# Two feed-forward units ordered by a table, squares moved into the loop, first projection by kind, first cast on VectorE

## The chip, the cores and the metric

The kernel runs on one core of one Trainium2 chip. The metric is the device time of one execution in microseconds (us); the kernel before was run three times: 2028.01, 2030.51 and 2027.96 us, median 2028.01. Engines are named as in the profile: PE is TensorE (PEld its weight loads), DVE VectorE, ACT ScalarE, POOL GpSimd, SP the queue that issues most transfers.

## What is computed

One transformer block on a sequence of 512 rows of 2048 columns, in float32. Cut to what matters here:

```python
h = rmsnorm(x, g_attn)
proj = h @ w_in                       # q, k, v of 16 heads and the forget gates
...                                   # two kinds of attention, head norms
x = x + mixed @ w_out
h2 = rmsnorm(x, g_mlp)
u = relu(h2 @ w_up)                   # 2048 -> 8192
x = x + (u * u) @ w_down              # 8192 -> 2048
y = rmsnorm(x, g_final)
```

## The kernel before

**Products of float32.** TensorE is fed with operands split in two: a high part, which ScalarE makes by a rounding copy ("cast"), and a low part, the source less the high part, which VectorE makes ("low"). A product is then three matmuls, high by high (hh), high by low (hl) and low by high (lh), in `mm3` (lines 75 to 78). Split operands of weights go to rotating rooms (`hi_lo`, line 67): three of them, and more where `more_parts` has entries.

**Seven products for eight.** The large products are done as one level of Winograd's scheme: two by two blocks on both sides, seven products numbered 1 to 7 instead of eight, with sums of blocks on either side. Sums of weights are made in place by VectorE (`Unit.source`, `sums_ahead`), sums of the left side by `a_source`; `left_form` and `a_form` split a sum of the left side into its high and low form `F[p]`.

**Three places matter here.**

*The first projection (lines 212 to 444).* x comes in as 16 chunks of 128 columns. For chunk k, `turn_x` transposes it on TensorE into one of two banks; from that bank ScalarE writes hH (`x_high`), VectorE hL (`x_low`), and further copies and sums are taken for later products (`x_more` on VectorE; `x_right` on ScalarE and `x_sum` on VectorE for chunks 8 to 15). The bank is free for the chunk after next when all of them have read it. Then the chunk is multiplied with its rows of the first weights: `first_part` does all four row blocks of one kind, hh, hl or lh, with the three kinds at 0, 0.6 and 1.1 us of the plan; `first_values` does two row blocks with the three kinds in turn. The first eight chunks of `seq` use `first_part`, the last eight `first_values`. `keep_busy(n)` puts n dummy matmuls into a spare bank. `square_x` takes sums of squares of x on ScalarE. The whole stage is a `Plan`: a list of jobs with times, sorted by time and then traced, inside a block where TensorE, ScalarE, VectorE and SP keep the order of the trace (`manual_schedule`). The times only order the jobs; nothing waits for a clock. The next stage, the values of the other heads, begins with products of pieces named `q` into the bank `vx`.

*The first two feed-forward units (lines 1612 to 1636).* A unit is 256 columns of w_up. Units 0 and 1 are multiplied while the last left forms are still being made, as plain products of 24 matmuls each into banks A, B and C (`psa`, `psb`, `psc`), in the order 1, 2 for each unit and then 5, 6, 7, 4, 3 with the units in turn. `product` makes the split, multiplies and calls `finish`, which copies banks out on ScalarE, adds them on VectorE, and after product 3 applies Relu and Square to the unit's result c. Before, the planner of the language orders these instructions by its own model, held back in places by `issue_after`. The last quarter of x, `quarter[1, 0]`, is turned in between (`turn_quarter`), stored to `xd`, and its squares are taken in place (`take_squares`).

*The loop over the other units (lines 1709 to 1749).* Steps of 16 matmuls, one product each, in an order fixed by hand on TensorE, ScalarE and VectorE: at step k the cast of step k + 3, the low of step k + 2, the sum of step k + 4 (`step_cast`, `step_low`, `step_source`), the copies and sums of step k - 1, Relu and Square of a finished unit one per step (`later`), and the forms of finished pairs of units, which are stored to memory for the down projection (`todo`, `going`, `form_low`: seven forms for a pair, each a sum where there is one, a cast, a low and a store). Loads of w_up go to `rw`, five rooms; the result c of units 0 and 1 takes one of them until its forms are made. SP is not held to an order here.

Of the kernel before, what the change touches and what calls it, by code (L numbers as in the profile page):

```python
# [14 lines left out]
P = 128  # L15
# [21 lines left out]
def block_kernel(ctx, tc, x, g_attn, w_in, b_f, g_out_sb, g_out_fox, w_out, g_mlp, w_up, w_down, g_final, y):  # L37
# [117 lines left out]
    class Piece:  # L155
# [13 lines left out]

        def low(self):  # L170
            lows[0] = dve.tensor_tensor(self.lo, self.source(), self.hi.bitcast(F32), op=ALU.subtract)
# [40 lines left out]
    with ExitStack() as stage:  # L212
# [82 lines left out]
        def first_part(j, piece, i, part):  # L295
            for t in range(TB):
                ts = slice(t * P, (t + 1) * P)
                a, b = (hH[j], piece.hi) if part == "hh" else (hH[j], piece.lo) if part == "hl" else (hL[j], piece.hi)
                pe.matmul(first_ps[t][:, :m], a[:, ts], b[:, i, :], start=j == 0 and part == "hh", stop=False, skip_group_check=True)
# [43 lines left out]
        for j in seq[:8]:  # L343
            for part, wait in zip(("hh", "hl", "lh"), (0.0, 0.6, 1.1)):
                plan.at(mm_at[j] + wait, first_part, j, *pieces[j], part)
        plan.at(-58.0, keep_busy, 9)
        plan.at(-54.5, keep_busy, 1)
        plan.at(1.0, keep_busy, 5)
        early = {0: ((-5.0, turn_x), (-4.1, "cast"), (-4.0, x_high), (-3.9, "low"), (-3.5, x_low), (-3.3, x_more)),
# [4 lines left out]
                 10: ((-2.36, turn_x), (-1.4, x_high), (-0.7, x_low), (0.05, x_sum), (0.55, x_right)),  # L354
# [8 lines left out]
        for k in range(4, K8):  # L363
            t, j = mm_at[k], k + K8
            for jj, dt in ((k, 0.0), (j, step)):
                for half in range(2):
                    plan.at(t + dt + 0.74 * half, first_values, jj, *pieces[jj], half)
# [792 lines left out]

    class Unit:
        def __init__(self, u):
            self.u = u
            cols = slice(2 * u * P, 2 * (u + 1) * P)
            rows_ = w_up.rearrange("(a i p) f -> i p a f", i=2, p=P)
            self.rows = rows_[0][:, :, cols], rows_[1][:, :, cols]
            self.b = []
            if u >= 2:
                self.load(0)
                self.load(1)  # L1170
            self.A = None
            self.both = u >= 2
            self.summed = False
# [7 lines left out]
        def sums_ahead(self):  # L1181
            (b11, b12), (b21, b22) = self.b
            dve.tensor_tensor(b11, b12, b11, op=ALU.subtract)
            dve.tensor_tensor(b12, b22, b12, op=ALU.subtract)
            self.summed = True

        def source(self, p):
# [5 lines left out]
            if p == 4:  # L1193
                with ExitStack() as order_:
                    if self.summed:
                        order_.enter_context(tc.issue_after(lows[0].ins))
                    dve.tensor_tensor(b21, b21, b11, op=ALU.subtract)
# [40 lines left out]
        def product(self, p):  # L1238
            ins = self.multiply(p, self.parts(p))
            self.finish(p)  # L1240
            return ins

# [35 lines left out]
        def finish(self, p):  # L1278
            if self.both:
                self.copies(p)  # L1280
                self.sums(p)
                if p == 3:
                    for _ in self.squares():
                        pass
                return
            if p == 2:
                if self.u % 2 == 0:
                    hidden[0] = rw.tile([P, 2, 2, NT], F32, tag="rw", name="c")
                self.pair = hidden[0]
                self.c = hidden[0][:, self.u % 2]  # L1290
            t1, t2 = slice(0, 2 * P), slice(2 * P, NT)
            if p in (1, 6, 7):
# [4 lines left out]
                if p == 1:  # L1297
                    self.m1 = self.m
            if p == 7:
                dve.tensor_tensor(self.c[:, 1, t2], self.m, self.C, op=ALU.add)  # L1300
            if p == 2:
                dve.tensor_tensor(self.c[:, 0, t1], self.m1, self.B, op=ALU.add)
            if p == 4:
                act.copy(self.c[:, 0, t2], self.A)
            if p == 3:
                dve.tensor_tensor(self.c[:, 1, t1], self.m6, self.C, op=ALU.add)
                act.activation(self.c, self.c, AF.Relu)
                act.activation(self.c, self.c, AF.Square)
# [67 lines left out]

    def turn_quarter(t0, j, db):
# [4 lines left out]
        for a in range(2):  # L1382
            tr = trp.tile([P, 2, 2 * P], F32, tag="tr", name="tr1")
            for i in range(2):
                for t in range(2):
                    pe.transpose(tr[:, i, t * P:(t + 1) * P], x_[:, t, (2 * a + i) * P:(2 * a + i + 1) * P], ident)
            for i in range(2):
                k = 4 * n + 2 * a + i
                act.mul(hr[db][j][:, a, i, t0 * 2 * P:(t0 + 1) * 2 * P], tr[:, i, :], g_up[:, k:k + 1])
# [5 lines left out]
    def take_squares():  # L1395

        t0, n, x_ = squares.pop(0)
        for t in range(2):
            act.activation(x_[:, t, :], x_[:, t, :], AF.Square, accum_out=ss2[:, 2 * t0 + t, n:n + 1])
# [7 lines left out]
    for db in range(2):  # L1407
# [204 lines left out]
    ins = units[0].multiply(1, begun[0])  # L1612
    with tc.issue_after(ins.ins):
        turn_quarter(1, 0, 1)
    units[0].multiply(2, begun[1])
    units[0].finish(1)
    units[0].finish(2)
    for p in (1, 2):
        ins = units[1].product(p)
    for unit in units[:2]:  # L1620
        unit.sums_ahead()
    left_form(4, 1, 0)
    left_form(5, 1, 0)
    for p in (5, 6, 7, 4, 3):
        for j in range(2):

            with tc.issue_after(ins.ins):
                ins = units[j].product(p)
            q = {5: 6, 6: 7, 7: 3}.get(p)
            if q is not None:  # L1630

                with tc.issue_after(lows[0].ins):
                    if (q, j) != (6, 0):
                        left_form(q, 1, 1 - j)
    while squares:
        take_squares()
# [15 lines left out]
    todo += [(q, hidden[0], 0) for q in A_ORDER]  # L1652
# [45 lines left out]
    going, later, pair_next = [], [], None  # L1698
# [10 lines left out]
    with tc.manual_schedule(engines={pe.engine, act.engine, dve.engine}):  # L1709
        for k in range(3):  # L1710

            for step in (step_source, step_cast, step_low):
                step(k)
        step_source(3)
        for k in range(len(steps)):
# [29 lines left out]
            if n in (1, 3, 6, 5 if steps[k][0] % 2 else 2) or steps[k][0] < 4:  # L1745
# [250 lines left out]
```

## Time and profile before

| what | value |
|---|---|
| median of three runs | 2028.01 us |
| the profiled execution | 2029.46 us |
| its span, first to last instruction | 2027.7 us |
| DVE, ACT busy | 1739.6 and 1128.6 us |
| HBM traffic | 315.19 MB read, 96.49 MB written |
| first projection | about 6.5 to 39.5 us of the span |
| units 0 and 1 | about 775.9 to 818.4 us |
| loop over the other units | from 818.4 us |

A row of a timeline gives the start in us, the duration in us, the engine, the line, the operation, what it writes and reads, shapes, a count, and in brackets how long the engine had been idle before it and what ended that. Matmuls overlap, so their spacing is read from the starts. A row of waits gives the total in us, how often, and the longest. Rows of windows give the busy time of each engine and the number of its instructions in a stretch.

### The profile page before, as it was taken

The page shows a single profiled execution, that of the slowest core. Times are in us where ns is not written, and L with a number is a line of the kernel's source. Part 1 is how long each engine was busy: PE and PEld are TensorE (multiplying, and loading weights), DVE is VectorE, ACT ScalarE, POOL GpSimd, SP SyncE. Part 2 cuts the span into 40 slices and gives each one's busy share as a digit, 9 for nine tenths or more (in the row PEclk, how much of TensorE's full clock was granted, in tenths as well). Part 3 has the DMA queues.
Part 4 walks back from the last instruction along what each step waited for, and adds up shares of the span by engine and source line. Part 5 has one row for each costly group of instructions (what it writes and reads, how often), then busy time and mean ns, then how long its engine had stood idle before and what let it go on. Part 6 is the DMA issues. An engine that isn't in the chain of part 4 may idle for free.

```text
span 2027.7 us, 27207 instructions
## 1 busy us (share of the span) xinstructions
PE 2016.1 (99%) x10425; PEld 1745.7 (86%) x10425; DVE 1739.6 (86%) x1970; ACT 1128.6 (56%) x1619; POOL 63.6 (3%) x72
## 2 busy tenths in 40 slices
PE   9999999999999999999999999999999999999998
PEld 9998888888898889888888888888888888888886
DVE  7886777888868588999999999998798888888896
ACT  7544444555555556666767767676644344444344
POOL 0000110100000000000000000000000000000004
PEclk9999999999999999999999999999999999999999
DMA  7427656666648981666676666666785574674642
GB/s 241 165 72 253 216 189 196 192 210 184 192 140 275 300 270 64 220 185 198 197 217 187 209 207 190 215 196 241 254 312 191 220 265 167 231 256 175 217 159 84
DMA packets 270179, 413.46 MB, mean 204 GB/s; under 512 B 10280, under 2 KB 165976, under 8 KB 263520
## 3 DMA queue, kind: packets, MB, share of 16 engines
q1 hardware_dynamic: 269296, 409.61, 60.7%
q8 instruction: 82, 1.34, 0.3%
q10 hardware_dynamic: 752, 2.11, 0.3%
q14 instruction: 49, 0.40, 0.1%
HBM read 315.19 MB, written 96.49 MB: 203 GB/s over the span
## 4 chain that ended last, share of the span: by engine, by line
PE 95%; DVE 3%; ACT 1%; issue 1%; DMA 0%; ACTq 0%
PE psa L1229 10%; PE accd L78 8%; PE accd L77 8%; PE accd L76 8%; PE accq L76 6%; PE accq L78 6%; PE accq L77 6%; PE psa L1227 5%; PE psc L1229 5%; PE psc L1227 3%; PE psb L1229 3%; PE m L77 1%; PE m L78 1%; PE m L76 1%; PE psb L1227 1%; PE vy L78 1%
## 5 line engine op out<-in xcount | busy, mean ns | idle before, releaser
L1806 ACT CAST wh<-wd 128x1024 fp32r<-128x1024 f32 x126 | 125.1, 999 | 168.2 <-PE accd L78 55.1
L1696 DVE TENSOR_TENSOR wl<-wu,wh 128x1024 fp32r<-128x1024 f32 x158 | 192.6, 1220 | 13.0 <-ACT wh L1690 13.0
L76 PE MATMUL accq<-hH,wh 128*128 128x512 f32 x512 | 201.4, 393 | 0.0
L78 PE MATMUL accq<-hH,wl 128*128 128x512 f32 x512 | 199.7, 390 | 0.0
L77 PE MATMUL accq<-hL,wh 128*128 128x512 f32 x512 | 199.6, 390 | 0.0
L1690 ACT CAST wh<-wu 128x1024 fp32r<-128x1024 f32 x158 | 167.4, 1060 | 44.8 <-issue 22.6
L1229 PE MATMUL psa<-f,wh 128*128 128x512 f32 x720 | 179.0, 391 | 0.0
L77 PE MATMUL accd<-wl,uf 128*128 128x512 f32 x436 | 169.6, 389 | 0.0
L78 PE MATMUL accd<-wh,uf 128*128 128x512 f32 x436 | 169.6, 389 | 0.0
L76 PE MATMUL accd<-wh,uf 128*128 128x512 f32 x436 | 169.4, 389 | 0.0
L1229 PEld LDWEIGHTS psa<-f,wh 128*128 128x128 f32 x720 | 132.3, 188 | 25.6
L1813 DVE TENSOR_TENSOR wl<-wd,wh 128x1024 fp32r<-128x1024 f32 x126 | 144.0, 1151 | 10.6 <-ACT wh L1806 10.6
L1578 DVE TENSOR_TENSOR m<-m,accd 128x1024 f32<-128x1024 f32 x84 | 102.2, 1217 | 47.7 <-PE accd L78 47.7
L1806 ACT CAST wx<-wd 128x1024 fp32r<-128x1024 f32 (+1 forms) x82 | 80.8, 995 | 107.4 <-PE accd L78 43.5
L78 PEld LDWEIGHTS accq<-hH,wl 128*128 128x128 f32 x512 | 96.1, 188 | 20.1
L77 PEld LDWEIGHTS accq<-hL,wh 128*128 128x128 f32 x512 | 96.2, 188 | 18.6
L76 PEld LDWEIGHTS accq<-hH,wh 128*128 128x128 f32 x512 | 96.3, 188 | 18.5
L76 PE MATMUL accd<-wx,uf 128*128 128x512 f32 x284 | 110.5, 389 | 0.0
L77 PE MATMUL accd<-wx,uf 128*128 128x512 f32 x284 | 110.5, 389 | 0.0
L78 PE MATMUL accd<-wx,uf 128*128 128x512 f32 x284 | 110.5, 389 | 0.0
L168 ACT CAST wh<-wraw 128x1024 fp32r<-128x1024 f32 (+1 forms) x70 | 72.8, 1041 | 60.1 <-PE accq L77 51.2
L1227 PEld LDWEIGHTS psa<-f,wl 128*128 128x128 f32 x720 | 96.0, 191 | 5.9 <-ACT l L1260 0.6
(445 smaller groups left out, 5104.2 us busy)
## 6 DMA issues: line engine op xcount, KB each, us to landing
wu<-in_w_up_dram SPq DMA_DIRECT2D x60, 1024.0 KB, 6.5
ufd<-st SPq DMA_DIRECT2D x98, 512.0 KB, 3.8
wd<-in_w_down_dram SPq DMA_DIRECT2D x48, 1024.0 KB, 8.3
uf<-ufd SPq DMA_DIRECT2D x42, 1024.0 KB, 6.7
wraw<-in_w_in_dram SPq DMA_DIRECT2D x68, 512.0 KB, 4.1
wo<-wsums SPq DMA_DIRECT2D x28, 512.0 KB, 5.0
q<-in_w_in_dram SPq DMA_DIRECT2D x32, 384.0 KB, 6.3
wd<-in_w_down_dram SPq DMA_DIRECT2D x16, 768.0 KB, 5.8
```

The source lines that it names most:

```text
L76: pe.matmul(out, sh, mh, start=first, stop=False, skip_group_check=True)
L77: pe.matmul(out, sh, ml, start=False, stop=False, skip_group_check=True)
L78: return pe.matmul(out, sl, mh, start=False, stop=last, skip_group_check=True)
L168: act.copy(self.hi, self.source())
L1227: ins = pe.matmul(ps[:, 2 * P:], lo[:, a, :], f_parts(p, a)[0], start=False, stop=last, skip_group_check=True)
L1229: ins = pe.matmul(ps, hi[:, a, :], f_both(p, a), start=a == PAIRS[0] and p in (1, 5), stop=last, skip_group_check=True)
L1578: dve.tensor_tensor(M[p][:, :, db, :], M[p][:, :, db, :], ps, op=ALU.add)
L1690: act.copy(rooms[k][0], srcs[k])
L1696: lows[0] = dve.tensor_tensor(lo, srcs.pop(k), hi.bitcast(F32), op=ALU.subtract)
L1806: act.copy(rooms[k + 3][0], srcs[k + 3])
L1813: dve.tensor_tensor(rooms[k + 2][1], srcs.pop(k + 2), rooms[k + 2][0].bitcast(F32), op=ALU.subtract)
```

## The change

1. The high part of the weights of chunk 0 is made by VectorE (`cast_dve`) instead of ScalarE, and one dummy matmul of five before the first product is dropped.
2. `first_values` is gone: all 16 chunks are multiplied by `first_part`, one kind after the other.
3. `x_right` of chunk 10 stands directly behind its `x_high` instead of 1.85 us later in the plan.
4. Units 0 and 1 become a `Plan` of their own, with every cast, low, sum, multiply, copy and addition at a time, in a block that holds TensorE, ScalarE and VectorE to the order. `finish` is split for these units into `copied` (ScalarE) and `added` (VectorE). The transposes of the last quarter come after the second product instead of between the first and the second, and its squares later among the casts. The left sum of product 7 for the second half is made ahead of the first products.
5. The addition after product 3 of units 0 and 1 is made among the first lows of the loop, and their Relu and Square go through the loop's list, one per step. The forms of this pair are queued only after them, and the rule by which the first units' steps each took a form is dropped.

```diff
+        def cast_dve(self):
+            self.hi, self.lo = (w.rearrange("p (a b) -> p a b", a=self.a) for w in hi_lo(self.a * self.b))
+            dve.tensor_copy(self.hi, self.source())
...
-                pe.matmul(first_ps[t][:, :m], a[:, ts], b[:, i, :], start=j == 0 and part == "hh", stop=False, skip_group_check=True)
-
-        def first_values(j, piece, i, half):
-            for t in (2 * half, 2 * half + 1):
-                ts = slice(t * P, (t + 1) * P)
-                mm3(first_ps[t][:, :m], hH[j][:, ts], hL[j][:, ts], piece.hi[:, i, :], piece.lo[:, i, :], j == 0, j == KC - 1)
+                pe.matmul(first_ps[t][:, :m], a[:, ts], b[:, i, :], start=j == 0 and part == "hh", stop=j == KC - 1 and part == "lh", skip_group_check=True)
...
-        for j in seq[:8]:
+        for j in seq:
...
-        plan.at(1.0, keep_busy, 5)
-        early = {0: ((-5.0, turn_x), (-4.1, "cast"), (-4.0, x_high), (-3.9, "low"), (-3.5, x_low), (-3.3, x_more)),
+        plan.at(1.0, keep_busy, 4)
+        early = {0: ((-5.0, turn_x), (-4.1, "cast_dve"), (-4.0, x_high), (-3.9, "low"), (-3.5, x_low), (-3.3, x_more)),
...
-                 10: ((-2.36, turn_x), (-1.4, x_high), (-0.7, x_low), (0.05, x_sum), (0.55, x_right)),
+                 10: ((-2.36, turn_x), (-1.4, x_high), (-1.3, x_right), (-0.7, x_low), (0.05, x_sum)),
...
+            with tc.issue_after(lows[0].ins):
+                summed[7, 1, 1] = a_source(7, hr[1][1])
             with tc.issue_after(casts[0].ins):
                 begun = [units[0].parts(1), units[0].parts(2)]
+            for p in (5, 7):
+                units[0].sum_ahead(p)
...
+    plan, groups = Plan(), {}
+    last = (1, 0, 1)
+    plan.at(-2.9, units[0].multiply, 1, begun[0])
+    plan.at(0.0, units[0].multiply, 2, begun[1])
+    for a in range(2):
+        plan.at(2.95, lambda a=a: groups.update({a: turn_group(*last, a)}))
+        plan.at(4.05 + 0.95 * a, lambda a=a: take_group(*last, a, groups[a]))
+        plan.at((14.0, 19.7)[a], lambda a=a: take_square(1, 1, quarter[1, 0], a))
+    plan.at(2.96, lambda: sp.dma_start(xd[1][:, 2:4, :], quarter[1, 0]))
+
+    for u, p, begin_, total, cast, low in (
+            (1, 1, 3.8, None, -1.9, -0.8), (1, 2, 6.7, None, 0.5, 3.4), (0, 5, 9.75, None, 3.0, 4.65), (1, 5, 12.45, None, 7.2, 8.5),
+            (0, 6, 16.05, 10.4, 11.65, 12.85), (1, 6, 18.2, 11.6, 12.9, 14.8), (0, 7, 21.1, None, 15.6, 17.4), (1, 7, 24.0, None, 18.6, 19.3),
+            (0, 4, 26.9, 20.5, 21.8, 23.0), (1, 4, 29.8, 21.75, 24.4, 25.1), (0, 3, 32.7, None, 27.3, 29.2), (1, 3, 35.6, None, 30.2, 30.9)):
+        w = FirstProduct(u, p)
...
+    for p, j, total, cast, low in ((7, 1, None, -1.0, 1.5), (4, 0, None, 5.95, 7.1), (5, 0, 7.8, 8.45, 9.7), (6, 0, 14.1, 14.85, 16.0),
+                                   (7, 0, 16.7, 17.45, 18.6), (3, 1, 24.2, 25.5, 26.35), (3, 0, 27.0, 28.4, 28.5)):
+        w = Left(p, j)
...
+    for t, f, u, p in ((0.1, "copied", 0, 1), (6.2, "added", 0, 2), (6.8, "copied", 1, 1), (12.5, "added", 1, 2), (18.25, "copied", 0, 6),
+                       (21.15, "copied", 1, 6), (24.05, "copied", 0, 7), (24.9, "added", 0, 7), (26.95, "copied", 1, 7),
+                       (27.7, "added", 1, 7), (29.85, "copied", 0, 4), (32.75, "copied", 1, 4)):
+        plan.at(t, getattr(units[u], f), p)
+    for t, p in ((2.2, 5), (5.9, 7)):
+        plan.at(t, units[1].sum_ahead, p)
+    with tc.manual_schedule(engines={pe.engine, act.engine, dve.engine}):
+        plan.run()
...
-    todo += [(q, hidden[0], 0) for q in A_ORDER]
...
-    going, later, pair_next = [], [], None
+    going, later, pair_next = [], [w.squares() for w in units], units[1]
...
+            if k == 2:
+                units[0].added(3)
             for step in (step_source, step_cast, step_low):
                 step(k)
...
             step_cast(k + 3)
+            if k == 0:
+                units[1].added(3)
...
             if later and next(later[0], 1):
-                later.pop()
+                later.pop(0)
...
-            if n in (1, 3, 6, 5 if steps[k][0] % 2 else 2) or steps[k][0] < 4:
+            if n in (1, 3, 6, 5 if steps[k][0] % 2 else 2):
                 form_low()
```

The new classes `Left` and `FirstProduct` hold one job each: `sum` is the sum of blocks (VectorE), `cast` the high part (ScalarE), `low` the low part (VectorE), `multiply` the 24 matmuls. In the first list of the table, the columns are unit, product, and the times of multiply, sum, cast and low.

More of the change, by code (lines that the diff above doesn't have):

```diff
@@ L1159, in a_form @@
         split(*out, a_source(p, c, s))
+    summed = {}
     class Unit:
@@ L1278, in finish, with copied @@
         def finish(self, p):
[L1279 to L1291, printed above, removed]
+            self.copies(p)
+            self.sums(p)
+            if p == 3:
+                for _ in self.squares():
+                    pass
+        def copied(self, p):
             if p in (1, 6, 7):
@@ L1382, in turn_quarter @@
         for a in range(2):
[L1383 to L1389, printed above, removed]
+            take_group(t0, j, db, a, turn_group(t0, j, db, a))
         sp.dma_start(xd[n][:, 2 * t0:2 * t0 + 2, :], x_)
@@ L1609, in block_kernel @@
     old = None
[L1612 to L1634, printed above, removed]
@@ L1635, in block_kernel, with __init__, sum, cast @@
-    while squares:
-        take_squares()
+    class Left:
+        def __init__(self, p, j):
+            self.p, self.c, self.at = p, hr[1][j], slice(2 * j, 2 * j + 2)
+        def sum(self):
+            self.src = a_source(self.p, self.c)
+        def cast(self):
+            if self.p == 4:
+                self.sum()
+            if F[self.p][1] is None:
+                F[self.p][1] = form.tile([P, 4, 2, 2 * P], F32R, tag=f"fl{self.p}", name=f"f{self.p}")
+            self.out = [F[self.p][1][:, self.at, c, :] for c in range(2)]
+            act.copy(self.out[0], self.src)
+        def low(self):
+            lows[0] = dve.tensor_tensor(self.out[1], self.src, self.out[0].bitcast(F32), op=ALU.subtract)
@@ new lines, in block_kernel, with __init__, sum, cast @@
+    class FirstProduct:
+        def __init__(self, u, p):
+            self.unit, self.p, self.src = units[u], p, None
+        def sum(self):
+            self.src = self.unit.source(self.p)
+        def cast(self):
+            if self.src is None:
+                self.sum()
+            self.parts = self.unit.room(self.p)
+            act.copy(self.parts[0], self.src)
+        def low(self):
+            lows[0] = dve.tensor_tensor(self.parts[1], self.src, self.parts[0].bitcast(F32), op=ALU.subtract)
+        def multiply(self):
+            self.unit.multiply(self.p, self.parts)
@@ new lines, in block_kernel @@
+    plan, groups = Plan(), {}
[8 more added lines that the diff above has]
+    for u, p, begin_, total, cast, low in (
[3 rows of a table added]
+        w = FirstProduct(u, p)
+        if total is not None:
+            plan.at(total, w.sum)
+        for t, f in ((cast, w.cast), (low, w.low), (begin_, w.multiply)):
+            plan.at(t, f)
```

60 lines of the change are left out of this document (37 added, 23 removed).

## The prediction

> **What bounds the kernel now.** I read the page's shares first, then the chain, then what TensorE and its weight loads (PEld) waited for over the whole span, and last the timelines around those few waits.
>
> ```profile
> PE 2016.1 (99%) x10425; PEld 1745.7 (86%) x10425; DVE 1739.6 (86%) x1970; ACT 1128.6 (56%) x1619; POOL 63.6 (3%) x72
> PE 95%; DVE 3%; ACT 1%; issue 1%; DMA 0%; ACTq 0%
> PEld psa L78 <- DVE wl L59: 1.0, 2, 0.5
> PEld vy L78 <- DVE hL L262: 0.6, 3, 0.2
> PEld psa L1227 <- ACT l L1260: 0.6, 1, 0.6
> PEld tr L256 <- ACT x L268: 0.4, 1, 0.4
> ...
> ```
>
> TensorE is busy 99% of the span, and the chain that ended last is 95% TensorE. So work taken off another engine is worth nothing in itself; only a TensorE gap can be won. 2027.7 less 2016.1 leaves 11.6 us without a matmul, head and tail included, and the waits (total us, times, longest) name four gaps that lie where the edits are: at most 2.6 us. That is the first answer: this change can win two or three microseconds, about 0.1%.
>
> ```profile
> core 0: us, PE busy (x) PEld busy (x) DVE busy (x) ACT busy (x) POOL busy (x), PEclk, DMA share, GB/s
> 10.20:39.46 29.26, 29.00 (x237) 28.20 (x237) 25.35 (x41) 23.16 (x42) 0.00 (x0) 1.00 0.75 268
> 32.00:36.00 4.00, 3.98 (x34) 3.77 (x33) 4.00 (x7) 2.78 (x5) 0.00 (x0) 1.00 0.54 186
> 775.90:818.40 42.50, 41.86 (x347) 41.46 (x346) 37.57 (x47) 24.58 (x39) 0.00 (x0) 1.00 0.34 109
> ```
>
> The third stretch is the two units that go into the table: 347 matmuls in 42.5 us, 0.12 us each, with VectorE at 37.57 of 42.5 and ScalarE at 24.58. Neither is full there; only their order can hurt.
>
> **The change part by part. First weights cast on VectorE, four dummy matmuls for five.**
>
> ```profile
> 4.39 1.05 PE L256 MATMUL tr<-ident,xa 128*128 128x128 f32 x4
> 6.50 0.81 PE L299 MATMUL vy<-wh,hH 128*128 128x264 f32 x2
> 8.84 0.64 PE L299 MATMUL vz<-wl,hH 128*128 128x264 f32 x2
> 9.28 0.64 PE L299 MATMUL vy<-wh,hL 128*128 128x264 f32 x2
> 5.45 0.41 ACT L168 CAST wh<-wfirst 128x264 fp32r<-128x264 f32 x1 [2.88 <-DMA wfirst<-in_w_in_dram]
> 5.77 0.68 ACT L259 ACTIVATE hH<-tr,g_in 128x512 fp32r<-128x512 f32 x1
> 1.23 0.29 DVE L289 CAST still<-f 128x256 fp32r<-128x256 f32 x1
> 5.89 0.43 DVE L171 TENSOR_TENSOR wl<-wfirst,wh 128x264 fp32r<-128x264 f32 x1 [1.60 <-ACT wh L168]
> ```
>
> The first product starts at 6.50, when the high part of x is done (5.77 + 0.68 = 6.45). That instruction stood behind the cast of the weights; x itself was turned by 4.39 + 1.05 = 5.44. On VectorE, idle for 1.60 us there, the cast costs about 0.3 (nearest row: 256 columns in 0.29) and ends near 5.8, when wl could start before as well. ScalarE then starts at about 5.46, and the product at 6.18, 0.32 earlier; the dropped dummy matmul makes room for that. But matmuls in this stretch start 0.22 apart (8.84 to 9.28 for two) against 0.12 later, so 0.32 us of them is 0.32 x 0.12 / 0.22 = **0.17** of later time, if the pace still changes at the same moment. Bounds: 0 (if the VectorE cast delays wl) and 0.32.
>
> [...]
>
> **x_right of chunk 10 right behind its x_high.**
>
> ```profile
> 19.41 0.40 PE L299 MATMUL vz<-wh,hL 128*128 128x264 f32 x2
> 20.03 0.66 PE L256 MATMUL tr<-ident,xa 128*128 128x128 f32 x4 [0.22 <-ACT x L268]
> 19.50 0.48 ACT L268 ACTIVATE x<-tr,g_in 128x256 f32<-128x256 f32 x1
> ```
>
> Turning chunk 11 needs the bank of chunk 10, whose last reader is this x_right at 19.50. TensorE loses 20.03 - 19.41 - 2 x 0.12 = **0.38**. Moved ahead of a square and a cast, x_right ends near 17.5, and nothing else reads the bank so late. Queued behind it on ScalarE, the square and the next x_high (18.39) slip by some 0.2, and that chunk's product starts only after 20; on VectorE, chunk 10's x_low slips by up to 0.3, and its lh are the last of the chunk (the row at 19.41). Both are covered. Bounds: 0 and 0.38.
>
> **All chunks by kind.** The last eight chunks ran hh, hl, lh for each pair of blocks; now every chunk runs its four hh, then four hl, then four lh.
>
> ```profile
> 36.17 0.28 PE L77 MATMUL vy<-wl,hH 128*128 128x264 f32 x1
> 36.48 0.39 PE L78 MATMUL vy<-wh,hL 128*128 128x264 f32 x1
> 29.37 0.75 DVE L262 SCALAR_TENSOR_TENSOR hL<-tr,g_in,hH 128x512 fp32r<-128x512 f32 x1 [0.23 <-ACT x L268]
> 37.34 0.75 DVE L262 SCALAR_TENSOR_TENSOR hL<-tr,g_in,hH 128x512 fp32r<-128x512 f32 x1 [0.26 <-ACT x L268]
> 38.40 1.82 DVE L171 TENSOR_TENSOR wl<-q,wh 128x768 fp32r<-128x768 f32 x2
> ```
>
> The third matmul of a chunk waited for hL: 36.48 - 36.17 - 0.12 = 0.19 here, three times in all, so **0.5** by the longest (PEld says 0.6). By kind, hL is wanted at the ninth matmul, 6 x 0.12 = 0.7 us later than at the third, and every one of these waits is under 0.2. The number of matmuls and their 0.12 stay. Bounds: 0.3 and 0.6.
>
> What is late next is VectorE: full from 32 to 36 (4.00 of 4.00), it makes the first wl of the next stage at 38.40, done at 38.40 + 1.82 / 2 = 39.31; TensorE begins that stage at 39.46 and needs wl one matmul later. Coming 0.17 + 0.38 + 0.5 = 1.05 earlier it would want wl at about 38.6. If VectorE did not move, 0.7 would be given back. But both ends of its full run wait on ScalarE (0.23 at 29.37, 0.26 at 37.34), and ScalarE there waits for the turned chunk from TensorE: the run moves with TensorE by about 0.55 at its head, and the gap at its end takes the rest. I take **0.05** given back; bounds 0 and 0.7.
>
> **The two units in a table.**
>
> ```profile
> 805.89 0.28 PE L77 MATMUL psa<-f,wh 128*128 128x256 f32 x1
> 806.46 0.38 PE L78 MATMUL psa<-f,wl 128*128 128x256 f32 x1 [0.29 <-DVE wl L59]
> 802.80 1.22 DVE L1197 TENSOR_TENSOR wu<-wu 128x1024 f32<-128x1024 f32 x1
> 818.44 2.00 PE L1229 MATMUL psa<-f,wh 128*128 128x512 f32 x8
> ```
>
> Product 4 of each unit waits for wl, 806.46 - 805.89 - 0.12 = 0.45, twice: **0.9**. Its sum was started on VectorE only at 802.80. In the table sum, cast and low of unit 0's product 4 stand 6.4, 5.1 and 3.9 us ahead of its multiply. The work is the same (12 casts, 12 lows, 7 left forms and so on), so VectorE's 37.57 of 42.5 stays. Of the leads, added up from durations in the table's order, the thinnest is this: low of left form (5, 0) comes after some 9.5 us of VectorE work from -0.8, ending about 10.5, and is wanted by the 19th matmul of product (0, 5) at 9.75 + 18 x 0.12 = 11.9; every other low stands two or more us ahead. Rooms: each cast comes after the multiply three before it, by the table. The transposes of the last quarter move from between the first two products to behind them, the same eight; its two squares wait for the store of x, issued at about 3 on SP, which the table does not order, and stand at 14.0 and 19.7. Bounds: 0 (another instruction is late in the new order) and 1.0 (the PEld row).
>
> **Squares and left forms in the loop.**
>
> ```profile
> 843.55 1.98 PE L1229 MATMUL psa<-f,wh 128*128 128x512 f32 x8
> 848.12 0.42 DVE L1269 TENSOR_TENSOR c<-c,psc 128x256 f32<-128x256 f32 x1
> 853.56 1.06 ACT L1276 ACTIVATE c<-c 128x1024 f32<-128x1024 f32 x1
> 855.20 0.98 PE L1227 MATMUL psa<-f,wl 128*128 128x256 f32 x6 [0.37 <-ACT l L1260]
> 825.45 0.69 DVE L1508 TENSOR_TENSOR st<-c,st 128x512 fp32r<-128x512 f32 x1 [0.51 <-ACT st L1506]
> 843.99 0.68 DVE L1508 TENSOR_TENSOR st<-c,st 128x512 fp32r<-128x512 f32 x1
> ```
>
> Nine steps of the loop take 843.55 - 818.44 = 25.1, 2.79 each. VectorE adds a finished bank (848.12) 4.6 us after TensorE left it (843.55): it has made the seven forms of the first pair one per step, 825.45 to 843.99. Relu and Square follow late on ScalarE, the copies stand behind the Square of 853.56, and TensorE loses 0.37. With the condition on steps below 4 gone, forms come at four per unit, begin at the fourth step (behind two Relu and two Square at one per step) and end near the 15th, 818.44 + 15 x 2.79 = 860. By step 8 three instead of seven are done: four times 0.68, and the sums before three of them, off VectorE, over 3 us of the 4.6. So the **0.37** goes. The two additions into c now stand on VectorE between the loop's first lows, and block them until the last table products end: then sum, cast, low of step 2 (1.2 + 1.0 + 1.2) are done some 4 us on, against 5.6 until TensorE's third step. Bounds: -0.5 (the forms now crowd steps 8 to 15) and 0.4.
>
> **The sum:** 0.17 + 0.38 + 0.5 - 0.05 + 0.9 + 0.37 = 2.27, so the span goes from 2027.7 to 2025.4 and the profiled execution from 2029.46 to 2027.2. The median of the three runs, 2028.01, lies 1.45 below the profiled one; taken from it, **2025.7 us**. Nothing between 40 and 775 or after 870 eats it: TensorE has next to no waits there.
>
> **The rivals.**
>
> 1. *VectorE sets the end of the first stage.* For: 4.00 of 4.00 busy there. Against: its run starts and ends on ScalarE waits that come earlier. It gives back 0.7 instead of 0.05: 2028.01 - 1.6 = 2026.4.
> 2. *The table gains nothing*, because only the order is fixed and another low comes as late as the old one. For: VectorE 88% busy. Against: the leads above. Without the 0.9 and the 0.37: 2027.0.
> 3. *The pace changes earlier* relative to the first product. For: the slow stretch from 6.50 to about 10.2 costs 3.7 x (1 - 0.12 / 0.22) = 1.7 us that no row ties to the edit. Against: nothing in the edit moves it on purpose. 2025.7 - 1.7 = 2024.0.
> 4. *Slower: weight loads queue behind form stores on SP.* The loop's loads and the stores of forms share SP in order, and the forms move from steps 1 to 7 into steps 4 to 15, where the fifth room of the weights also stays with c.
>
> ```profile
> 840.62 0.38 SPq L1179 DMA_DIRECT2D wu<-in_w_up_dram  x1
> wu<-in_w_up_dram SPq DMA_DIRECT2D x60, 1024.0 KB, 6.5
> ```
>
> The load at 840.62 is unit 4's second half, there at 847.2, and its first reader (a sum for step 16, taken at step 12) comes at 818.44 + 12 x 2.79 = 851.9: 4.7 us of cover. Unit 5's second half loses c's room and must wait for unit 3's, at about 858, there at 864.5 against 871.4. If a load stands behind a store whose form is one place later, two steps, 5.6 us, TensorE loses 0.9; from 4.7 + 2.3 = 7.0 us on the kernel is slower than before, and with two such places, 11.2 us, it loses 6.5: 2028.01 - 2.3 + 6.5 = 2032.2. Against: the loads become ready by VectorE's own pace, which is better now.
>
> **How the numbers follow.** Forecast 0.56 (2024.6 to 2026.9 by its bounds and the runs' spread), rival 1 0.13, rival 2 0.10, rival 3 0.10, rival 4 0.11. A measurement of this kernel can tell about 0.2%, 4.06 us, from no change: 2023.95 to 2032.07. Half of rival 3 lies below, with a little of the forecast: faster 0.07. Rival 4 is above in most of its cases: slower 0.08. Same 0.85. The range takes the forecast, rivals 1 and 2 and most of 3: 2023.9 to 2029.2; the upper end leaves room for the spread of the runs (those before reach 2030.51).
>
> **What would show it.** First product near 6.2 with the same 0.22 spacing up to about 10; no TensorE gap before the transposes at about 19.6 and none at third matmuls of chunks; the next stage starting near 38.5, with or without a wait for wl (rival 1). The two units ending about 41.6 us after they begin instead of 42.6, with no weight load waiting for wl. VectorE's addition of a bank at the ninth step within about 1.5 us of TensorE's end instead of 4.6, and no wait behind L1260. A TensorE wait on a load of wu in the 40 us after the loop begins would make rival 4 right, a span over 2027.7 would make the whole sum wrong.

## The result, and the profile after

| | before | after |
|---|---|---|
| median, 15 runs each | 2028.59 us | 2024.33 us |
| lowest to highest | 2027.82 to 2030.51 us | 2024.07 to 2024.92 us |
| ratio, 95% interval | | 0.9979 (0.9971 to 0.9987) |
| the profiled execution, its span | 2029.46, 2027.7 us | 2024.44, 2022.7 us |

The changed kernel is 4.26 us faster, 0.21%, where 2.3 us were forecast: the direction and the range held, but the forecast was little more than half of the gain. The page after, with busy times and the chain, then what TensorE's weight loads waited for over the whole span:

```profile
PE 2013.0 (100%) x10424; PEld 1743.7 (86%) x10424; DVE 1739.4 (86%) x1971; ACT 1127.2 (56%) x1618; POOL 63.1 (3%) x72
PE 100%; ACT 0%; DVE 0%; issue 0%; ACTq 0%
```

```profile
PEld vx L297 <- DVE still L293: 1.6, 1, 1.6
PEld trg L252 <- issue: 0.5, 2, 0.2
PEld trb L719 <- DVE rw L714: 0.4, 1, 0.4
PEld accoa L78 <- DVE g L59: 0.4, 1, 0.4
PEld tr L260 <- issue: 0.3, 1, 0.3
PEld vy L303 <- ACT hH L263: 0.2, 1, 0.2
```

The chain is now TensorE alone. The waits for hL, for the weights' low parts in the units (psa L78) and for the copies in the loop are all gone. One row is new: tr L260 is a short wait before the next transposes, those of chunk 4 (the run e8 below is about it). No wait for a load of wu has come in.

Where the time came from is read by cutting the span at the same five matmuls in each kernel: the first product, chunk 1's first product, chunk 11's transposes, the first matmul of the next stage, the first of the units, the first of the loop; the last piece ends with TensorE. The windows of the changed kernel (bounds, length, busy us and instructions of each engine), then the first and last matmul of the loop's piece and the last store:

```profile
core 0: us, PE busy (x) PEld busy (x) DVE busy (x) ACT busy (x) POOL busy (x), PEclk, DMA share, GB/s
6.23:8.57 2.34, 2.34 (x18) 2.32 (x17) 1.79 (x4) 0.93 (x2) 0.00 (x0) 1.00 1.04 321
8.57:18.15 9.58, 9.58 (x82) 9.53 (x81) 8.32 (x15) 7.81 (x15) 0.00 (x0) 1.00 1.06 390
18.15:36.93 18.78, 18.61 (x159) 18.43 (x157) 17.59 (x28) 15.47 (x29) 0.00 (x0) 1.00 0.73 247
773.40:814.81 41.41, 41.41 (x347) 41.41 (x346) 36.99 (x46) 23.65 (x38) 0.00 (x0) 1.00 0.35 113
814.81:2014.71 1199.90, 1199.90 (x6086) 1026.28 (x6084) 1100.31 (x1147) 681.98 (x954) 20.13 (x14) 1.00 0.62 208
...
```

```profile
814.81 2.00 PE L1225 MATMUL psa<-f,wh 128*128 128x512 f32 x8
2014.43 0.28 PE L78 MATMUL acce<-ws,us 128*128 128x256 f32 x1
2018.34 0.39 ACTq L1977 DMA_DIRECT2D out_dram<-last  x1
```

In the units and in the loop TensorE is busy for every hundredth of the stretch: 41.41 of 41.41 and 1199.90 of 1199.90. In the stretch from 18.15 a hole of 0.17 us is left. The end of the profile before:

```profile
2018.68 0.28 PE L78 MATMUL acce<-ws,us 128*128 128x256 f32 x1
2022.62 0.40 ACTq L1922 DMA_DIRECT2D out_dram<-last  x1
```

TensorE ends 4.25 us earlier. The span shrank by 5.0: from the issue of the last store to the end it is 2022.7 - 2018.34 = 4.4 us now and 2027.7 - 2022.62 = 5.1 before, which no step of the prediction had.

The lengths of all pieces, for these two profiles and for those of the experiments below (the stretch between the next stage and the units is 736.4 to 736.5 us in all but one, 736.7):

| profile | first product to chunk 1 | chunk 1 to 11 | 11 to next stage | units | loop to TensorE's end | last store to end |
|---|---|---|---|---|---|---|
| before | 3.66 | 9.87 | 19.43 | 42.56 | 1200.52 | 5.12 |
| e9_before | 2.49 | 9.97 | 19.43 | 43.03 | 1200.53 | 5.16 |
| e10_before | 2.00 | 10.06 | 19.44 | 43.14 | 1200.54 | 5.12 |
| e1_start | 2.49 | 9.61 | 18.77 | 42.91 | 1200.51 | 4.36 |
| e2_units | 2.01 | 10.78 | 19.43 | 41.41 | 1199.90 | 4.36 |
| e3_cast | 2.00 | 9.97 | 19.45 | 43.05 | 1200.50 | 5.11 |
| e4_kind | 2.44 | 9.60 | 18.78 | 42.90 | 1200.51 | 4.37 |
| e5_xright | 2.31 | 9.61 | 19.74 | 42.61 | 1200.68 | 4.35 |
| e6_forms | 1.99 | 10.09 | 19.44 | 42.92 | 1199.90 | 4.38 |
| after | 2.34 | 9.58 | 18.78 | 41.41 | 1199.90 | 4.38 |
| e12_after | 2.22 | 9.61 | 18.75 | 41.41 | 1199.90 | 4.37 |
| e11_old_head | 2.58 | 9.59 | 18.75 | 41.42 | 1199.89 | 4.38 |
| e7_old_forms | 2.61 | 9.58 | 18.77 | 41.42 | 1201.13 | 4.66 |
| e8_bank | 2.42 | 9.61 | 18.40 | 41.41 | 1199.90 | 4.36 |

In the new order the pieces repeat within 0.04 us, and so do the third column (19.43 to 19.45) and the loop (1200.50 to 1200.54) of the old order; the one exception in the loop is e5 with 1200.68, for which no further gap on TensorE was found. In such a column an edit's effect shows to the tenth. The first column doesn't repeat at all. In the old order the second runs from 9.87 to 10.09, with one 10.78, and the units' from 42.56 to 43.14.

### The profile page after: what moved, and what is told of

It reads as the page before. It is cut to its first block, busy times and chain, and to the rows that moved or that the text cites. A ratio compares the mean times of both kernels' runs of the same rounds, so it can differ in the third digit from the quotient of the medians.

```text
span 2022.7 us, 27206 instructions
## 1 busy us (share of the span) xinstructions
PE 2013.0 (100%) x10424; PEld 1743.7 (86%) x10424; DVE 1739.4 (86%) x1971; ACT 1127.2 (56%) x1618; POOL 63.1 (3%) x72
## 4 chain that ended last, share of the span: by engine, by line
PE 100%; ACT 0%; DVE 0%; issue 0%; ACTq 0%
PE psa L1225 11%; PE accd L76 8%; PE accd L78 8%; PE accd L77 8%; PE accq L76 6%; PE accq L78 6%; PE accq L77 6%; PE psa L1223 6%; PE psc L1225 5%; PE psc L1223 3%; PE psb L1225 3%; PE psb L1223 1%; PE m L76 1%; PE m L78 1%; PE m L77 1%; PE accoa L78 1%
## 5 line engine op out<-in xcount | busy, mean ns | idle before, releaser
L78 PE MATMUL accq<-hH,wl 128*128 128x512 f32 x512 | 199.7, 390 | 0.0
L78 PE MATMUL accd<-wh,uf 128*128 128x512 f32 x436 | 169.6, 389 | 0.0
L78 PEld LDWEIGHTS accq<-hH,wl 128*128 128x128 f32 x512 | 96.1, 188 | 20.2
L78 PE MATMUL accd<-wx,uf 128*128 128x512 f32 x284 | 110.5, 389 | 0.0
```

The source lines that it names most:

```text
L78: return pe.matmul(out, sl, mh, start=False, stop=last, skip_group_check=True)
```

## The experiments

Each was timed beside the kernel before on the same chip, in five rounds (11 runs each, before 21 or 33) except e9 and e10, one run each. The medians of the kernel before were 2028.58 for e1 to e4, 2028.54 for e5 to e8, 2028.50 for e9 to e12. The times of e1, e3, e4, e5 and e6 have intervals that reach 1 or nearly so; for these the stage lengths carry the reading, not the ratio.

**The two halves apart.** e1 is the kernel before with the edits to the first projection alone (the diff down to the eight later chunks' first_values); e2 has only those to units and loop.

> The kernel before with only the edits of the first projection (VectorE cast and four dummy matmuls, all chunks by kind, x_right of chunk 10 earlier). If the gains simply add, 2.5 us of the 4.3 come from here: about 0.9988 of the time before. If the earlier change of TensorE's pace was chance, it is 1.2 us (0.9994) and the slow stretch ends near 10 us again.

> The kernel before with only the table for units 0 and 1, the squares in the loop's list and the slower rate of forms. If each removed wait also saves a restart of the next matmul (0.1 us each), the span is 1.15 + 0.64 = 1.8 us shorter (0.9991); if only the waits as I summed them count, 0.9 + 0.37 = 1.3 us (0.9994).

e1: 2026.74 us, 0.9991 (0.9982 to 1.0000). e2: 2025.47 us, 0.9986 (0.9977 to 0.9994). The gains, 1.84 and 3.11, add up to 4.95, 0.69 more than the whole change. The table shows what both contain: the last column falls from 5.1 to 4.36 in each, 0.75 us that the whole change can have only once. Without it e1 gains 1.1 and e2 2.4. For e1 that is the lower of the two expected gains, in which the earlier change of pace was chance; for e2 it is more than either, since the units of the first profile before were short (42.56). Each half acts in its own pieces: e1 in the second and third, e2 in the units and the loop. But e2's second piece, which it leaves as it was, is 10.78. What the weight load before chunk 11's transposes waited for in that execution, and ScalarE's timeline there:

```profile
PEld tr L256 <- ACT x L268: 1.2, 1, 1.2
```

```profile
18.04 0.63 ACT L168 CAST wh<-wfirst 128x528 fp32r<-128x528 f32 x1 [0.68 <-DMA wfirst<-in_w_in_dram]
18.57 0.47 ACT L268 ACTIVATE x<-tr,g_in 128x256 f32<-128x256 f32 x1
```

x_right of chunk 10 (L268) stood in order behind a cast that waited 0.68 us for its weights to land, and TensorE's wait for the bank became 1.2 us instead of 0.4. So in the old order a late transfer could reach TensorE through an instruction that doesn't read it.

**The parts of the first half.** e3 has the VectorE cast and the four dummies alone, e4 everything of the first half but these, e5 the moved x_right alone.

```
e3:  def cast_dve(self): ... dve.tensor_copy(self.hi, self.source())
     plan.at(1.0, keep_busy, 5)  ->  plan.at(1.0, keep_busy, 4)
     0: (..., (-4.1, "cast"), ...)  ->  0: (..., (-4.1, "cast_dve"), ...)
e4:  after's first_part for all of seq, no first_values, x_right early;
     keep_busy 5 and "cast" as before
e5:  10: (..., (-1.4, x_high), (-0.7, x_low), (0.05, x_sum), (0.55, x_right))
 ->  10: (..., (-1.4, x_high), (-1.3, x_right), (-0.7, x_low), (0.05, x_sum))
```

> The kernel before with only the cast of chunk 0's weights on VectorE and four dummy matmuls for five. Theory 1: these move the moment at which TensorE's matmuls go from 0.22 to 0.12 us apart, from about 10.2 to about 7 us: 1.6 us shorter (0.9992). Theory 2: that moment has nothing to do with them: first product 0.3 us earlier, 0.17 us shorter (0.9999), the slow stretch ending anywhere.

> The kernel before with only the chunks by kind and the earlier x_right. Theory 1: the slow stretch ends near 10.2 as before, and the gain is 0.37 + 0.95 less what VectorE gives back, about 1.0 us (0.9995). Theory 2: the slow stretch ends anywhere.

> The kernel before with only x_right of chunk 10 directly behind its x_high. Theory 1 (the gains of the first projection add): what by-kind and x_right gave together, 2.1 us, less the 0.95 of the hL waits, so about 1.1 us (0.9995), and no TensorE wait before chunk 11's transposes even where the cast in front waits for its weights to land. Theory 2 (the next wait eats it): hL, on VectorE, does not come earlier, and the gain is under 0.4 us (0.9998 or more).

e3: 2028.49 us, 1.0000 (0.9992 to 1.0009), no gain; its first theory, 1.6 us from an earlier change of pace, falls. e4: 2026.46 us, 0.9990 (0.9982 to 0.9999); of its 2.12, 0.75 stands in the last column, and the second and third piece together are 1.0 to 1.1 shorter than in e9 and e10, where 1.0 was expected. e5: 2027.42 us, 0.9996 (0.9987 to 1.0005). The windows of e5's second and third piece (columns as above), and its timeline at the next transposes (TensorE, then VectorE):

```profile
8.62:18.23 9.61, 9.61 (x82) 9.57 (x81) 8.35 (x15) 7.79 (x15) 0.00 (x0) 1.00 1.06 386
18.23:37.97 19.74, 19.53 (x158) 18.75 (x157) 17.81 (x28) 15.70 (x29) 0.00 (x0) 1.00 0.70 238
...
```

```profile
19.39 0.40 PE L299 MATMUL vz<-wl,hH 128*128 128x264 f32 x2
19.96 0.63 PE L256 MATMUL tr<-ident,xb 128*128 128x128 f32 x4 [0.17 <-issue]
```

```profile
18.50 0.70 DVE L171 TENSOR_TENSOR wl<-wfirst,wh 128x528 fp32r<-128x528 f32 x1
19.11 0.74 DVE L265 TENSOR_SCALAR x<-tr,g_in 128x512 f32<-128x512 f32 x1
```

The gap before chunk 11's transposes is gone, 9.61 against 9.87 to 10.09. But the third piece grew by 0.31: the transposes of chunk 4 at 19.96 start 0.33 later than two matmuls after 19.39 would let them. Their bank is that of chunk 3, whose last reader is x_more on VectorE at 19.11, done at 19.85, and VectorE has no gap from 17.84 up to it; e8 below shows that this is the cause. The time won at one bank was lost at the next: moved alone, x_right is worth about 0.1 us at the next stage (second and third column together are 29.35 in e5, and 29.30 to 29.53 in the five profiles with the old code in both pieces, e2 with its late transfer left out). So e5's median gain of 1.1 is the number that its first theory gave, but 0.75 of it stands in the last column; by the pieces the second theory, under 0.4, is right. Against e5's 19.74, the third piece of e4 and e1 is 18.78 and 18.77: multiplying by kind is worth 0.97.

**The bank of chunk 4.** e8 is the changed kernel with x_more of chunk 3 placed ahead of the low of chunk 4's weights on VectorE.

```
 3: (..., (-0.73, x_low), (0.0, x_more))  ->  3: (..., (-0.73, x_low), (-0.1, x_more))
```

> The changed kernel with x_more of chunk 3 put ahead of the low of chunk 4's weights on VectorE. In the profile after, the transposes of chunk 4 start 0.33 us late, right behind the end of this x_more. If VectorE holds the bank there, the gap goes and the time is 0.3 us below the kernel after (0.9977 to 0.9978 of before); if that gap came from a transfer, nothing changes (0.9979).

The window of its third piece, and TensorE's timeline at the same transposes:

```profile
18.26:36.66 18.40, 18.40 (x158) 18.40 (x157) 17.49 (x28) 15.44 (x29) 0.00 (x0) 1.00 0.74 250
...
```

```profile
19.42 0.40 PE L303 MATMUL vz<-wl,hH 128*128 128x264 f32 x2
19.66 0.60 PE L260 MATMUL tr<-ident,xb 128*128 128x128 f32 x4
```

The transposes follow 0.24 behind 19.42, and TensorE is busy for all of 18.40 us. The piece is 0.37 shorter, and the kernel runs 2024.02 us, 0.9978 (0.9969 to 0.9987), 0.31 below the changed one's median and so the fastest of all; that difference is no larger than the spread of either, and the 0.37 of the piece, which repeats to 0.03, carries it. In its profile no piece from chunk 1 on is longer than the changed kernel's by more than 0.03.

**The form rate in the loop.** e6 is the kernel before with the condition on steps below 4 dropped and nothing else; e7 is the changed kernel with it put back.

```
-            if n in (1, 3, 6, 5 if steps[k][0] % 2 else 2) or steps[k][0] < 4:
+            if n in (1, 3, 6, 5 if steps[k][0] % 2 else 2):
```

> The kernel before with only the condition on steps below 4 dropped, so that the first pair's forms come four to a unit. Theory 1: the forms at one per step made VectorE late; the wait at the loop's 13th step goes, 0.64 us with its restart (0.9997). Theory 2: Relu and Square in front of the loop made ScalarE late; the wait stays, no change (1.0000).

> The changed kernel with the condition on steps below 4 put back, so that the forms of the first pair, queued after the squares, come at one per step of units 2 and 3. Against the kernel after (0.9979 of before): theory 1, the wait behind the copies is back, 0.6 us more (0.9982); theory 2, as after (0.9979).

e6: 2027.04 us, 0.9993 (0.9984 to 1.0002). e7: 2025.64 us, 0.9986 (0.9977 to 0.9995), 1.31 over the changed kernel. The loop takes 1199.90 in e6, as in the changed kernel, so that one line alone takes the old order's 0.62 away. In e7 the loop takes 1201.13, worse than before; its ScalarE and TensorE there:

```profile
850.81 1.05 ACT L1267 ACTIVATE c<-c 128x1024 f32<-128x1024 f32 x1
851.76 0.35 ACT L1250 COPY c<-psa 128x256 f32<-128x256 f32 x1
852.01 0.38 ACT L1251 COPY l<-psa 128x256 f32<-128x256 f32 x1
```

```profile
852.44 1.22 PE L1223 MATMUL psa<-f,wl 128*128 128x256 f32 x8 [0.98 <-ACT l L1251]
```

The same wait as before, for copies that stand on ScalarE behind an activation over the whole of c, and longer. So the new place of the squares and additions doesn't take the wait away; the lower rate of forms does, and the new order of the loop needs it.

**Before again, and the head.** e9 and e10 are the unchanged kernel; e12 is the changed one again; e11 is the changed one with ScalarE's cast and five dummies as before.

```
e11: plan.at(1.0, keep_busy, 4)  ->  plan.at(1.0, keep_busy, 5)
     0: (..., (-4.1, "cast_dve"), ...)  ->  0: (..., (-4.1, "cast"), ...)
```

> The kernel before, unchanged, profiled again. Seven other profiles with five different heads all left the 0.22 us spacing between 6.1 and 7.3 us; only the first profile of the kernel before left it at 10.2. If that was chance: left before 8 us here, TensorE in the next stage 0.9 to 1.9 us earlier than 39.46, and a wider wait before chunk 11's transposes or in units 0 and 1. If it belongs to this kernel: 10.2 us again. The last store's landing, 5.1 us after its issue in that profile against 4.4 in most others, is 4.4 here if it varies by chance.

> As the run before it, a second look at the same kernel, for the spread: by chance, the end of the slow stretch and the landing of the last store differ between the two; by the kernel, both agree with the first profile (10.2 and 5.1 us).

> The changed kernel with the cast of chunk 0's weights back on ScalarE and five dummy matmuls. Theory 1 (the cast's place is worth its 0.27 us or the 0.17 of the prediction): slower by that, 0.9980 of before. Theory 2 (the weights land early enough in most runs that ScalarE casts them before x is turned): as the kernel after, 0.9979.

> The changed kernel, unchanged, beside the one with the old head, on the same chip: 0.9979 of before, about 2024.3 us; slow stretch left before 8 us, last store landed 4.4 us after its issue.

e9: 2028.62, e10: 2028.29. e11: 2024.47 us, 0.9979 (0.9970 to 0.9988). e12: 2024.27 us, 0.9979 (0.9970 to 0.9987). e11 and e12 differ by 0.2 us, where each spreads over 0.9 or more: the head's edit has no effect that can be told. And the last store took 5.16 and 5.12 us in e9 and e10, where 4.4 was expected if it varied by chance: the 5.1 came again with the kernel before. The slow spacing, in turn, ended before 8 us in both, as expected of chance. Why the head does nothing, in e10's timeline (ScalarE, then TensorE):

```profile
4.92 0.41 ACT L168 CAST wh<-wfirst 128x264 fp32r<-128x264 f32 x1 [2.35 <-DMA wfirst<-in_w_in_dram]
5.46 0.69 ACT L259 ACTIVATE hH<-tr,g_in 128x512 fp32r<-128x512 f32 x1
```

```profile
5.10 0.93 PE L293 MATMUL vx<-still 128*128 128x256 f32 x5
6.20 0.51 PE L299 MATMUL vy<-wh,hH 128*128 128x264 f32 x2 [0.17 <-ACT hH L259]
6.55 0.41 PE L299 MATMUL vz<-wh,hH 128*128 128x264 f32 x2
...
8.20 0.49 PE L299 MATMUL vy<-wh,hH 128*128 128x264 f32 x2
```

With the old head, the weights landed at 4.92, were cast before x was turned, and hH started at 5.46, as early as the VectorE cast ever let it (5.48 or 5.49). In e9 the cast stood at 5.20 and hH at 5.52, 0.03 late. The first profile of the kernel before, with 5.45 for the cast and 6.50 for the product, was an execution with a late landing. And here the matmuls leave the slow spacing at about 5.4, among the dummies (five take 0.93 us), not at 10.2.

The window of e10's units, for the kernel before in another execution than the first, the two waits of product 4 in it, and the row of its weight loads over the whole span:

```profile
774.09:817.23 43.14, 42.16 (x347) 41.55 (x346) 37.63 (x47) 24.66 (x39) 0.00 (x0) 1.00 0.34 108
...
```

```profile
805.25 0.38 PE L78 MATMUL psa<-f,wl 128*128 128x256 f32 x1 [0.53 <-DVE wl L59]
808.73 0.39 PE L78 MATMUL psa<-f,wl 128*128 128x256 f32 x1 [0.36 <-DVE wl L59]
```

```profile
PEld psa L78 <- DVE wl L59: 1.6, 3, 0.7
```

These units take 0.58 longer than in the first profile: product 4 waits more, and a third wait for a low part, which the first profile doesn't have, comes in product 6 of unit 1, before its third matmul at 795.83 (by the starts, the waits are 0.69, 0.51 and 0.25). e9 has the same three. They begin 1.8 us earlier than in the first profile, but an earlier start doesn't settle it: e5's begin at 774.36 and take 42.61. What lengthens the waits in the old order stays open; in the new one, the units take 41.41 or 41.42 in all six profiles that have it. Which part of the new order does this, the times of the plan or the sum and transposes that moved, was not tried.

## Why the prediction was right, and where its sizes were off

The mechanism was right: TensorE bounds the kernel, and only its gaps could be won. They closed where they were looked for, and but for 0.3 us no other engine took over. The number was helped by luck. The measured 2024.33 lies below 2024.6 to 2026.9, the band that the prediction gave its own forecast, and nearest to rival 3's 2024.0; it is inside the range because room was left for that rival, and because the kernel before took 2028.59 this time: 4.26 less than the 2028.01 of the forecast would be 2023.75, just under the 2023.9. The part won on TensorE, 3.4 us, would by itself leave 2025.2, inside the band. The terms, against the changed kernel's own lengths and those of e9 and e10:

| step | predicted | measured |
|---|---|---|
| VectorE cast, four dummies | 0.17 | 0 |
| x_right of chunk 10 | 0.38 | 0.4 at its gap, 0.3 of it lost at chunk 4's bank |
| hL waits, by kind | 0.5 | 0.97 |
| VectorE gives back | -0.05, at the next stage's wl | none there |
| the table | 0.9 | 1.6 to 1.7; 1.15 against the first profile |
| the loop | 0.37 | 0.63 |
| the last store | not seen | 0.75 |

Without the head, the measured terms are 0.42 (10.02 - 9.60 by the means of the second column), 0.67, 1.67 and 0.63, together 3.4 on TensorE, and 0.75 for the last store: 4.15, where the medians of the runs taken with e12, 2028.50 and 2024.27, differ by 4.23.

**The head.** The step that failed is the premise that ScalarE's cast delays x: it did in the first profile, with the cast at 5.45 and hH at 5.77, but in e2, e9, e10 and e11, whose weights landed earlier and whose casts start between 4.86 and 5.20, hH starts between 5.46 and 5.52. One profile was taken for the rule. The sign that went with it failed too: the next stage began at 36.93, not near 38.5, and of these 2.53 us earlier than before 1.32 are the first column.

**By kind and the table, each under-sized in the same way.** A stall was costed as its wait. These rows of the profile before follow directly on the stalled matmuls at 36.48 and 806.46 that the prediction quotes:

```profile
36.70 0.28 PE L76 MATMUL vy<-wh,hH 128*128 128x264 f32 x1
...
806.68 0.28 PE L76 MATMUL psa<-f,wh 128*128 128x256 f32 x1
```

The next matmul starts 0.22 after the stalled one, not 0.12, so each stall costs 0.1 more than the wait. In the table that is 0.45 and 0.50 of waiting (the second from 809.32 to 809.94), and 0.2 (0.22 to the next start there as well, 810.16), together the 1.15 measured between the two first profiles. For hL the three waits are 0.18, 0.18 and 0.11 by the starts (matmuls at 32.35, 36.48 and 38.14), not 0.19 each, and 0.3 comes on top; with 0.08 at 30.40, where a third matmul came without a gap and the next one late all the same, that is 0.85 of the 0.97, and the last 0.1 isn't traced. So the ceiling of 2.6 us, which the prediction read from the waits alone, was no ceiling. What makes the next start late is not shown; 0.2 also stands between the first two matmuls behind the four transposes of a chunk, without a wait there (31.85 and 32.06 in the profile before). The rest of the table's gain is that the old order waited longer in every other profile than in the first.

**x_right and VectorE's part.** The gap closed as predicted. VectorE did give something back, 0.3 where 0.05 was taken, but not at the first wl of the next stage. That wl starts at 35.98 and the stage at 36.93, with no wait between its first matmuls:

```profile
35.98 1.81 DVE L175 TENSOR_TENSOR wl<-q,wh 128x768 fp32r<-128x768 f32 x2
```

```profile
36.93 0.34 PE L76 MATMUL vx<-wh,hH 128*128 128x384 f32 x1
37.10 0.34 PE L77 MATMUL vx<-wl,hH 128*128 128x384 f32 x1
```

The prediction asked what is late next at the end of VectorE's full run, and of chunk 11's bank only up to its own transposes; the next bank, 1.5 us on, held by a VectorE instruction, was where it had to look. So rival 1 named the engine and got place and size (0.7) wrong.

**The loop.** The wait went for the stated reason, as e6 and e7 show. VectorE's addition of a bank at the ninth step comes 1.1 us after TensorE left it, where up to 1.5 was foretold and 4.6 was shown before:

```profile
839.92 1.98 PE L1225 MATMUL psa<-f,wh 128*128 128x512 f32 x8
...
841.06 0.41 DVE L1260 TENSOR_TENSOR c<-c,psc 128x256 f32<-128x256 f32 x1
```

The size was read wrongly: 0.37 is the idle time in the row's bracket, where the other stalls were costed from start to start. At 806.46 in the prediction the bracket has 0.29 and the starts give 0.45, 0.16 more; 0.37, 0.16 and the 0.1 of the restart make 0.63, and the piece lost 0.62.

**The other rivals.** Rival 2 falls: the units take 41.41, where 41.6 was foretold for the forecast. Rival 4 falls: no TensorE wait on a load. Rival 3's size is in the two first profiles, 3.66 - 2.34 = 1.32 in the first column, but not its cause: e2, e9 and e10, with the head of before untouched, reached chunk 1 within 2.0 to 2.5 us as well. The first profile of the kernel before was late, and its execution 0.9 us above the median of its 15 runs.

**The chances.** 2024.33 lies inside 2023.95 to 2032.07, the limits within which the prediction called the times the same (0.85), but the gain against the kernel before in the same runs, 4.26, is just over the 4.06 us that it held to be tellable, and faster had been given 0.07. The interval of the ratio, 0.13 to 0.29% faster, reaches to both sides of 0.2%. With 0.1 more for each of six stalls (three for hL, two in the table, one in the loop), 0.16 for the loop's start to start and 0.75 for the last store, the same sum would have been 2.27 + 0.6 + 0.16 + 0.75 = 3.8.

## What to carry to other kernels

Cost a TensorE stall from start to start, and add the slower start of the matmul behind it, which is read from the next two starts (0.1 us a stall here). When a gap at one buffer is closed, go to the next buffer and ask who holds it and on which engine: here 0.3 of 0.4 us went there, and a change of 0.1 in one time of the plan got it back. Compare stages between fixed landmarks and profile the kernel before more than once: the one profile had a late head and short waits in the units, and both misled.

## What the runs showed of the hardware that was not expected

**The moment at which the pace changes.** By the starts of the first matmuls, dummies and transposes included, the spacing fell from about 0.22 to about 0.12 us between about 5.4 (e10, e3) and 7.7 us (e11) in nine profiles (after, e1 to e4, e9 to e12), a wider spread than the 6.1 to 7.3 that e9's expectation names, and at about 10.2 in the first profile of the kernel before. In the two first profiles the granted clock reads 1.00 in each stretch of 2 us from 4 to 12 us, before the change and after it. The head doesn't decide the moment: e10, among the earliest, and e11, the latest of the nine, both have the old one. It varies by 2.3 us in the nine and by 4.8 with the first profile; what sets it is not shown here. In the first column it is worth up to 1.7 us (1.99 to 3.66).

**The last store.** From its issue to the end of the span it took 5.1 us in four profiles (the first of the kernel before, e3, e9 and e10), 4.35 to 4.38 in nine others and 4.66 in e7, though the stores are the same. The DMA view from the last store's issue on, of e10 and then of e12:

```profile
DMA packets 577, 1.06 MB, mean 203 GB/s; under 512 B 64, under 2 KB 64, under 8 KB 576
...
q14 instruction: 1, 0.01, 0.4%
...
out_dram<-last ACTq DMA_DIRECT2D x1, 256.0 KB, 4.0
```

```profile
DMA packets 576, 1.05 MB, mean 238 GB/s; under 512 B 64, under 2 KB 64, under 8 KB 576
...
out_dram<-last ACTq DMA_DIRECT2D x1, 256.0 KB, 3.3
```

In e10 a packet of the instruction queue falls among the last store's packets; in e12 it had gone a microsecond before the issue. In the first profile of the kernel before, with 5.1 too, it starts 2.3 us after the issue, and in that of the changed kernel about 1.0 before it. By views with slices of a microsecond, such a packet had also gone before the issue in e1 and e11, with 4.4, and none had gone in the four microseconds before it in e3 and e9, with 5.1. What made 4.66 in e7 is not shown. That such a packet delays the store is argued from this order alone; what moves it was not tried, and edits far from the end (e5's one moved instruction, e6's one condition) changed it. So 0.75 of the 4.26 us is no merit of the steps that were planned, and its cause stays open.
